# A two-layer decoder trunk on one Trainium2 core: feature tiles computed by three 256-column matmuls per contraction step instead of one of 512 and one of 256, and a pair of tiles in one PSUM bank

## The chip, the core and the metric

The kernel runs on one core of one Trainium2 chip. The metric is the device time of one execution in microseconds, as the median of several. TensorE is called PE here (its weight loads are a row of their own, PEld), VectorE is DVE, ScalarE is ACT, GpSimd is POOL and SyncE, which issues most loads, is SP.

## What is computed

A decoder trunk of two layers on 256 positions of width 2048, in fp32. Each layer has an attention mixer (dilated windows and cross-attention into 256 memory tokens in layer 0, stick-breaking attention and the same cross-attention in layer 1), an output projection, and a gated MLP. Cut to what matters here:

```python
def reference(x, mem, norms, w_in_a, w_o_a, g_kv, w_kv, w_in_b, w_o_b,
              w_mem_kv, w_up, w_conv, b_conv, w_down):
    ...
    h = _rmsnorm(x, nrm[0])
    proj = h @ w_in_a[layer]
    ...

def _conv_ffn(h, w_up, w_conv, b_conv, w_down):
    S = h.shape[1]
    u = h @ w_up
    gate, val = jnp.split(u, 2, axis=-1)
    gp = jnp.pad(gate, ((0, 0), (CONV_WIDTH - 1, 0), (0, 0)))
    acc = b_conv + gp[:, CONV_WIDTH - 1:CONV_WIDTH - 1 + S] * w_conv[CONV_WIDTH - 1]
    for j in range(CONV_WIDTH - 1):
        acc = acc + gp[:, j:j + S] * w_conv[j]
    return (jax.nn.silu(acc) * val) @ w_down
```

The change touches products `h @ w` whose output is wanted with features on the partitions: the queries and keys of both layers, the memory keys, the memory queries, and a part of `h @ w_up`.

## The kernel before

**Three products for one.** An fp32 matrix is held as two float32r parts, high and low. A product of two matrices is high times high, low times high and high times low, summed in PSUM. ACT makes the high part of a weight (line 601, a cast) and DVE the low part (line 602, a subtraction), for pieces of 128x1024. The activations `h` lie in a tile of 16 steps (`kt`, 128 features each) by two parts by 256 positions, so that high and low of one step are 512 columns side by side.

**Feature tiles.** A tile of 128 output features by 256 positions has the weight as the stationary operand and `h` as the moving one, over 16 contraction steps. Before, each step had two matmuls: the weight's high part against both parts of `h` at once (512 columns, line 145, and for the last step line 148), and the weight's low part against the high part of `h` (256 columns, line 146). The 512 columns are a whole PSUM bank: its left half gathers the products with the high part of `h`, its right half those with the low part. So the finished tile is the sum of the two halves: ACT copies the right half out (line 149), and DVE adds the left half (line 150). Each tile takes a bank of its own, out of four called `ps_g`.

**Pairs.** `ws_pair` calls `ws_tile` for two tiles with a common 128x2x256 output, and may multiply the pair by a row of norms (line 188). `narrow`, at the start of each MLP, makes its gate and value tiles so and multiplies the gates by the norm in `gate` (line 829).

**Beside the wide products.** Five groups of 512 features of each MLP are made by `wide`, with fewer products of another form (line 128, all of 512 columns, in seven banks: four `ps_g` and three `ps_s`). Between its matmuls `ws_beside` makes the eight feature tiles of the next group, in two halves of eight contraction steps per round of `wide`; its matmuls are on line 163, its copy and addition on lines 175 and 176, and its bank is the one `ps_s` bank left. Here every instruction is pinned: PE, ACT, DVE and SP run them in the order in which the code writes them. What belongs to a finished pair (gate, convolution, SiLU, product, split) is put on a list, `behind`, of which `catch_up` takes one step twice a round; steps that prepare sums of `h` (lines 585 to 594, 293) are on the same list at the start of a layer's first wide group.

**Counts.** There are 160 feature tiles, 80 by `ws_tile` and 80 by `ws_beside`. That is 2560 contraction steps, each of one 512-column and one 256-column matmul. Everywhere else a scheduler orders the instructions; in `wide` the code does.

Of the kernel before, what the change touches and what calls it, by code (L numbers as in the profile page):

```python
# [14 lines left out]
ALU = mybir.AluOpType  # L15
AX = mybir.AxisListType

P = 128
D = 2048
S = 256  # L20
# [4 lines left out]
KT = D // P  # L25
# [20 lines left out]
class Body:  # L46
# [49 lines left out]
    def pin(self, ins):  # L96
        return self.tc.keep_in_program_order(ins) if self.pinned else ins
# [32 lines left out]
        mm(out, llo, rhi, start=False, stop=False)  # L130
        mm(out, lhi, rlo, start=False, stop=stop)

    def ws_tile(self, out, src, h):


        mm, nc = self.nc.tensor.matmul, self.nc
        b = self.bank()
        self.step()
        for half, (whi, wlo) in enumerate(self.piece(src)):
            for k in range(8):  # L140
                kt = half * 8 + k
                ks = slice(k * P, (k + 1) * P)
                both, one = h[2][:, kt, :, :].rearrange("p a t -> p (a t)"), h[0][:, kt, :]
                if kt < KT - 1:
                    mm(b, whi[:, ks], both, start=kt == 0, stop=False)  # L145
                mm(b[:, 0:S], wlo[:, ks], one, start=False, stop=False)  # L146
                if kt == KT - 1:
                    mm(b, whi[:, ks], both, start=False, stop=True)  # L148
        nc.scalar.copy(out, b[:, S:])
        nc.vector.tensor_add(out, b[:, 0:S], out)  # L150

    def ws_beside(self, out, src, h, done=None):


        raw = self.sb.tile([P, 2048], F32, name="raw", tag="raw", bufs=3)
        self.pin(self.nc.sync.dma_start(raw, src))
        parts = []
        for i in range(2):
            parts.append([self.sb.tile([P, 1024], F32R, name=k, tag=k, bufs=4) for k in ("whi", "wlo")])
            self.split(*parts[i], raw[:, i * 1024:(i + 1) * 1024])  # L160
            yield
        b = self.bank("s")
        mm = lambda *o, **k: self.pin(self.nc.tensor.matmul(*o, **k))  # L163
        for half, (whi, wlo) in enumerate(parts):
            for k in range(8):
                kt = half * 8 + k
                ks = slice(k * P, (k + 1) * P)
                both, one = h[2][:, kt, :, :].rearrange("p a t -> p (a t)"), h[0][:, kt, :]
                if kt < KT - 1:
                    mm(b, whi[:, ks], both, start=kt == 0, stop=False)  # L170
                mm(b[:, 0:S], wlo[:, ks], one, start=False, stop=False)
                if kt == KT - 1:
                    mm(b, whi[:, ks], both, start=False, stop=True)
            yield
        self.pin(self.nc.scalar.copy(out, b[:, S:]))  # L175
        self.pin(self.nc.vector.tensor_add(out, b[:, 0:S], out))  # L176
        if done:
            done()

    def ws_pair(self, src, h, out=None, before=None, R=None):  # L180

        out = self.pairtile() if out is None else out
        for j in range(2):
            if before:
                before(j)
            self.ws_tile(out[:, j, :], src[j], h)
        if R is not None:
            self.nc.vector.tensor_tensor(out, out, R().unsqueeze(1).to_broadcast([P, 2, S]), op=ALU.mult)
        return out

    def as_mm(self, banks, parts, lhs, pi, tiles=(0, 1)):

# [530 lines left out]
    def ffn(self, layer, h, each, filler=None, done=None, late=None):  # L723
        nc = self.nc
        up, uw, dn = (self.a["%s%d" % (k, layer)] for k in ("up", "uw", "dn"))
        r, R = {}, []
# [12 lines left out]
        def spread():  # L739
            if len(R) == 1:  # L740
                R.append(self.spread(R[0], "R"))
            return R[1]

        s, make = self.sums_of_h(h)
# [25 lines left out]
        def weights(ft):  # L770
            return [self.cols[:, cv + i * NFT + ft:cv + i * NFT + ft + 1] for i in range(4)]

        def conv(p, ga):

            pin, c = self.pin, self.pairtile()

            def straight():
                for j in range(2):
                    w = weights(2 * p + j)
                    pin(nc.scalar.activation(c[:, j, :], ga[:, j, :], AF.Identity, scale=w[2], bias=w[3]))  # L780

            def shifted():
                for j in range(2):
                    w = weights(2 * p + j)
                    for i in (1, 0):
                        d = 2 - i
                        pin(nc.vector.scalar_tensor_tensor(c[:, j, d:], ga[:, j, :S - d], w[i], c[:, j, d:],
                                                           op0=ALU.mult, op1=ALU.add))

            def silu():  # L790
                pin(nc.scalar.activation(c, c, AF.Silu))
                if layer == 0 and p == 2 * WIDE[-1] + 1:

                    self.tc.keep_in_program_order(
                        nc.scalar.preload_act_table_set("natural_log_exp_and_others"))

            return c, (straight, shifted, silu)

        def keep(p, c, val):

            g, o = p // 2, p % 2 * 2
            part = lambda i: room[g][i][:, o:o + 2, :]

            def product():
                self.pin(nc.vector.tensor_tensor(c, c, val, op=ALU.mult))

            def high():
                if g not in acts:
                    acts[g] = []
                    room[g] = self.sh([P, 4, S], F32R), self.sh([P, 4, S], F32R)  # L810
                self.pin(nc.scalar.copy(part(0), c))

            def low():
                self.pin(nc.vector.tensor_sub(part(1), c, part(0).bitcast(F32)))
                hi, lo = room[g]
                acts[g] += [(hi[:, o + j, :], lo[:, o + j, :]) for j in range(2)]

            return product, high, low

        def at_once(steps):  # L820
            for step in steps:
                step()

        room = {}
        place = lambda p: p - 2 * sum(v < p // 2 for v in WIDE)

        def gate(ga):
            Rb = spread().unsqueeze(1).to_broadcast([P, 2, S])
            self.pin(nc.vector.tensor_tensor(ga, ga, Rb, op=ALU.mult))

        def narrow(g):
            for p in (2 * g, 2 * g + 1):
                if p == 0:
                    ahead.extend(self.first_sums(uw[0], u) for u in range(2))
                w = place(p)
                ga = self.ws_pair(up[w, 0], h)
                if p == 0:

                    val = self.ws_pair(up[w, 1], h)
                gate(ga)  # L840
                c, steps = conv(p, ga)
                at_once(steps)
                if p:
                    val = self.ws_pair(up[w, 1], h)
                at_once(keep(p, c, val))

        def beside(g):

            st = {}

            def tile(p, i, j):
                if (i, j) == (0, 0):
                    st[p] = [self.pairtile() for _ in range(2)]
                ga, val = st[p]

                def done():
                    if i == 0:
                        st["c"], steps = conv(p, ga)
                        self.behind_this(lambda: gate(ga), *steps)
                    else:  # L860
                        self.behind_this(*keep(p, st["c"], val))

                return self.ws_beside(st[p][i][:, j, :], up[place(p), i][j], h, done if j else None)

            return [lambda p=p, i=i, j=j: tile(p, i, j)
                    for p in (2 * g, 2 * g + 1) for i in range(2) for j in range(2)]

        def turned(g, made, i):
# [12 lines left out]
            at_once(keep(2 * g + i, c, both[1]))  # L881

        narrow(0)
        made = []

# [316 lines left out]
```

## Time and profile before

| what | us |
|---|---|
| time, median of 3 runs (2202.1 to 2207.01) | 2202.43 |
| the profiled execution | 2204.87 |
| its span, first to last instruction | 2203.1 |
| PE busy (10962 matmuls) | 2184.6 |
| PEld busy (weight loads) | 1837.5 |
| DVE busy | 1651.4 |
| ACT busy | 1296.0 |
| POOL busy | 149.1 |

A row of a group of instructions names line, engine and operation, the tiles it writes and reads, its shapes and count, then its busy time in us, the mean duration of one in ns, and the engine's idle time before it with what ended it. A matmul's recorded duration holds its way through the array, so that one begins before the one before it has ended: how fast a stream of matmuls runs is read from the distance between starts. A row of the timeline or of the chain of waits gives a start in us, a duration, and what ran.

### The profile page before, as it was taken

The numbers are of one execution on the slowest core, as the hardware profiler recorded it, in microseconds if no ns is written. First come the engines' busy times: TensorE is split into PE (matmuls) and PEld (weight loads), VectorE is DVE, ScalarE is ACT, GpSimd is POOL, SyncE is SP. The second block draws the span as 40 slices with busy tenths as digits, with TensorE's granted clock in tenths as the row PEclk, the third lists the DMA queues.
The fourth block names the chain that finished last, engine by engine and source line by source line (L and its number), as shares of the span: only waits on it lengthen the run. The fifth ranks groups of instructions, "written<-read, shape, count | busy, mean of one in ns | idle before, by whom it ended". The sixth has DMA issues, their size and how long they took to land.

```text
span 2203.1 us, 28992 instructions
## 1 busy us (share of the span) xinstructions
PE 2184.6 (99%) x10962; PEld 1837.5 (83%) x10962; DVE 1651.4 (75%) x2175; ACT 1296.0 (59%) x1844; POOL 149.1 (7%) x168
## 2 busy tenths in 40 slices
PE   9999999999999999999999999999999999999998
PEld 7888888888888888888888888878888888888886
DVE  6566767987787868778874677569878878687886
ACT  7545656656565665665664554455666656656563
POOL 0000000010101001010100000000101010110100
PEclk9999999999999999999999999999999999999999
DMA  8755557696979979797745444576969798797974
GB/s 320 268 179 179 183 172 248 206 279 221 286 233 283 267 221 295 232 283 257 260 172 191 153 172 165 188 240 203 279 215 293 234 280 264 233 296 225 284 242 181
DMA packets 102380, 516.78 MB, mean 235 GB/s; under 512 B 10464, under 2 KB 10848, under 8 KB 61920
## 3 DMA queue, kind: packets, MB, share of 16 engines
q1 hardware_dynamic: 72288, 439.43, 56.1%
q0 software_dynamic: 29952, 75.51, 17.2%
q8 instruction: 86, 1.41, 0.2%
q14 instruction: 54, 0.44, 0.1%
HBM read 491.82 MB, written 23.07 MB: 234 GB/s over the span
## 4 chain that ended last, share of the span: by engine, by line
PE 96%; DVE 2%; issue 1%; DMA 0%; SPq 0%; ACT 0%; POOL 0%; POOLq 0%; DVEq 0%; ACTq 0%
PE ps_g L128 42%; PE ps_s L163 20%; PE ps_g L145 13%; PE ps_s L128 10%; PE ps_g L146 7%; PE ps_g L148 1%; PE ps_s L876 1%; DVE wlo L602 1%; PE ps_s L279 1%; DMA raw<-in_wmv_dram 0%; PE ps_s L330 0%; PE ps_s L357 0%; PE ps_s L436 0%; PE ps_s L393 0%; PE ps_s L454 0%
## 5 line engine op out<-in xcount | busy, mean ns | idle before, releaser
L602 DVE TENSOR_TENSOR wlo<-raw,whi 128x1024 fp32r<-128x1024 f32 (+1 forms) x758 | 867.0, 1163 | 337.1 <-ACT whi L601 328.5
L601 ACT CAST whi<-raw 128x1024 fp32r<-128x1024 f32 (+1 forms) x758 | 751.4, 1004 | 437.5 <-PE ps_g L128 207.3
L163 PE MATMUL ps_s<-h,whi 128*128 128x512 f32 x1280 | 462.6, 398 | 2.4 <-DVE qk L176 2.4
L128 PE MATMUL ps_g<-whi,sh 128*128 128x512 f32 x1488 | 464.3, 393 | 0.0
L145 PE MATMUL ps_g<-h,whi 128*128 128x512 f32 x1200 | 430.3, 401 | 0.8 <-DVE h L269 0.8
L163 PE MATMUL ps_s<-h,wlo 128*128 128x256 f32 x1280 | 347.1, 281 | 1.2 <-DVE wlo L602 1.1
L146 PE MATMUL ps_g<-h,wlo 128*128 128x256 f32 x1280 | 345.7, 280 | 0.0
L128 PEld LDWEIGHTS ps_g<-whi,sh 128*128 128x128 f32 x1488 | 277.6, 188 | 57.4
L128 PE MATMUL ps_g<-wlo,sh 128*128 128x512 f32 x744 | 291.7, 392 | 0.0
L163 PEld LDWEIGHTS ps_s<-h,whi 128*128 128x128 f32 x1280 | 241.2, 188 | 55.2 <-ACT x L601 3.2
L128 PE MATMUL ps_g<-whi,h 128*128 128x512 f32 x880 | 275.4, 394 | 0.6 <-ACT whi L601 0.6
L145 PEld LDWEIGHTS ps_g<-h,whi 128*128 128x128 f32 x1200 | 225.4, 188 | 52.1 <-DVE h L269 1.1
L163 PEld LDWEIGHTS ps_s<-h,wlo 128*128 128x128 f32 x1280 | 242.3, 189 | 16.0 <-DVE wlo L602 2.3
L146 PEld LDWEIGHTS ps_g<-h,wlo 128*128 128x128 f32 x1280 | 241.5, 189 | 6.4
L602 DVE TENSOR_TENSOR x<-sh,x 128x1024 fp32r<-128x1024 f32 x160 | 189.2, 1219 | 0.0
L128 PEld LDWEIGHTS ps_g<-whi,h 128*128 128x128 f32 x880 | 159.0, 188 | 34.3 <-ACT whi L601 1.1
L128 PE MATMUL ps_g<-wlo,h 128*128 128x512 f32 x440 | 172.8, 393 | 1.1 <-DVE wlo L602 1.0
L128 PEld LDWEIGHTS ps_g<-wlo,sh 128*128 128x128 f32 x744 | 139.7, 188 | 32.5
L601 ACT CAST x<-sh 128x1024 fp32r<-128x1024 f32 x160 | 160.8, 1050 | 0.3 <-DVE sh L647 0.3
L609 POOL DMA_DIRECT2D sh<-in_uw_dram x80 | 97.8, 1226 | 673.4 <-DMA sh<-in_uw_dram 347.7
L175 ACT COPY qk<-ps_s 128x256 f32<-128x256 f32 x80 | 29.9, 374 | 186.1 <-PE ps_s L163 186.1
L128 PE MATMUL ps_g<-x,h 128*128 128x512 f32 x480 | 137.6, 394 | 0.0
(180 smaller groups left out, 2135.8 us busy)
## 6 DMA issues: line engine op xcount, KB each, us to landing
raw<-in_up_dram SPq DMA_DIRECT2D x96, 1024.0 KB, 6.1
raw<-in_dn_dram SPq DMA_DIRECT2D x88, 1024.0 KB, 5.8
raw<-in_uw_dram SPq DMA_DIRECT2D x80, 768.0 KB, 7.3
sh<-in_uw_dram SPq DMA_DIRECT2D x80, 512.0 KB, 8.1
sh<-in_uw_dram POOLq DMA_DIRECT2D x80, 512.0 KB, 10.6
raw<-in_wqk_a_dram SPq DMA_DIRECT2D x24, 1024.0 KB, 4.8
yout<-sh POOLq DMA_DIRECT2D x32, 512.0 KB, 8.6
raw<-in_wo_b_dram SPq DMA_DIRECT2D x16, 1024.0 KB, 4.9
```

Of the source, the lines that this page charges most:

```text
L128: mm = lambda *o, **k: self.pin(self.nc.tensor.matmul(*o, **k))
L145: mm(b, whi[:, ks], both, start=kt == 0, stop=False)
L146: mm(b[:, 0:S], wlo[:, ks], one, start=False, stop=False)
L148: mm(b, whi[:, ks], both, start=False, stop=True)
L163: mm = lambda *o, **k: self.pin(self.nc.tensor.matmul(*o, **k))
L175: self.pin(self.nc.scalar.copy(out, b[:, S:]))
L279: self.nc.tensor.transpose(b[:, k * S + t * P:k * S + (t + 1) * P], self.x[:, t, kt * P:(kt + 1) * P], self.ident)
L601: high = self.pin(self.nc.scalar.copy(hi, of))
L602: low = self.pin(self.nc.vector.tensor_sub(lo, of, hi.bitcast(F32)))
L609: self.nc.gpsimd.dma_start(d.rearrange("p (a n) -> p a n", a=2), src[u][:, 1536:].unsqueeze(1).to_broadcast([P, 2, 512]), accum_op=ALU.add)
L876: nc.tensor.transpose(b[:, j * S + t * P:j * S + (t + 1) * P], of[t][:, f:f + P], self.ident)
```

## The change

Each contraction step of a feature tile becomes three matmuls of 256 columns into the same 256 columns of PSUM: weight high by `h` high, weight low by `h` high, weight high by `h` low. The sum of the three products is then complete in PSUM. Two tiles of a pair lie side by side in one bank, and one instruction takes the bank out: an ACT copy of 128x512, or, where the pair is multiplied by the norm, that DVE multiplication reading PSUM. The copy and addition for each tile go. In `ws_beside` the bank is taken at the pair's first tile, nothing is taken out after that tile, and the gate multiplication comes at once behind the pair's last matmul, where before it was a step on the list `behind`.

```diff
-    def ws_tile(self, out, src, h):
+    def ws_part(self, out, parts, h, half):
...
+        mm = lambda *o, **k: self.pin(self.nc.tensor.matmul(*o, **k))
+        whi, wlo = parts
+        for k in range(8):
+            kt = half * 8 + k
+            ks = slice(k * P, (k + 1) * P)
+            mm(out, whi[:, ks], h[0][:, kt, :], start=kt == 0, stop=False)
+            mm(out, wlo[:, ks], h[0][:, kt, :], start=False, stop=False)
+            mm(out, whi[:, ks], h[1][:, kt, :], start=False, stop=kt == KT - 1)
...
-        nc.scalar.copy(out, b[:, S:])
-        nc.vector.tensor_add(out, b[:, 0:S], out)
...
+        for j in range(2):
+            if before:
+                before(j)
+            self.step()
+            for half, parts in enumerate(self.piece(src[j])):
+                self.ws_part(b[:, j * S:(j + 1) * S], parts, h, half)
+        b = b.rearrange("p (j t) -> p j t", j=2)
+        if R is None:
+            self.nc.scalar.copy(out, b)
+        else:
+            self.nc.vector.tensor_tensor(out, b, R().unsqueeze(1).to_broadcast([P, 2, S]), op=ALU.mult)
+        return out
...
-        self.pin(self.nc.scalar.copy(out, b[:, S:]))
-        self.pin(self.nc.vector.tensor_add(out, b[:, 0:S], out))
-        if done:
-            done()
...
+        if j == 0:
+            st["b"] = self.bank("s")
+        for half in range(2):
+            self.ws_part(st["b"][:, j * S:(j + 1) * S], parts[half], h, half)
             yield
+        if j:
+            done(st["b"].rearrange("p (j t) -> p j t", j=2))
...
-                def done():
+                def done(b):
                     if i == 0:
+                        gate(ga, b)
                         st["c"], steps = conv(p, ga)
-                        self.behind_this(lambda: gate(ga), *steps)
+                        self.behind_this(*steps)
                     else:
+                        self.pin(nc.scalar.copy(val, b))
                         self.behind_this(*keep(p, st["c"], val))
```

In the changed kernel all matmuls of feature tiles are on line 135, the pair's copy and multiplication on lines 156 and 158, gate and copy of the tiles beside `wide` on lines 817 and 850, and the split of weights on lines 589 and 590.

On PE, at the first pair of memory keys in layer 0, these are the rows before, from the end of one tile into the next (`ps_g_287` and `ps_g_342` are two banks, `whi` and `wlo` the parts of a weight, `h1` the activations):

```order
L145 MATMUL ps_g_287<-h1_84,whi_294 128x512
L146 MATMUL ps_g_287<-h1_84,wlo_295 128x256 x2
L148 MATMUL ps_g_287<-h1_84,whi_294 128x512
L145 MATMUL ps_g_342<-h1_84,whi_345 128x512
L146 MATMUL ps_g_342<-h1_84,wlo_346 128x256
```

The same place after the change:

```order
L135 MATMUL ps_g_277<-h1_84,whi_294 128x256 x2
L135 MATMUL ps_g_277<-h1_84,wlo_295 128x256
L135 MATMUL ps_g_277<-h1_84,whi_294 128x256
L135 MATMUL ps_g_277<-h1_84,whi_358 128x256
L135 MATMUL ps_g_277<-h1_84,wlo_359 128x256
```

Every step has three matmuls of 256 columns now, and the second tile goes on in the bank of the first. What stands between the feature tiles on PE has kept its place, but for a few matmuls at three points.

On DVE, where the first wide group of layer 0 goes over from its first tile beside to the second, these are the rows before (`wlo<-raw,whi` is the low part of a weight, `qk` the pair's output or a scratch pair, `x<-sh,x` the low part of a sum of weights; the rows from `qk<-h` to the last `qk<-qk` and the one on `h_3298` prepare sums of `h`):

```order
L293 TENSOR_TENSOR h_3298<-qk,h_3298 128x4x128
L590 TENSOR_TENSOR qk<-h_2654 128x512
L592 TENSOR_TENSOR qk<-qk 128x128
L585 SCALAR_TENSOR_TENSOR qk<-qk 128x128
L594 TENSOR_TENSOR qk<-qk 128x128
L585 SCALAR_TENSOR_TENSOR qk<-qk 128x128
L176 TENSOR_TENSOR qk<-ps_s,qk 128x256
L602 TENSOR_TENSOR wlo<-raw,whi 128x1024 x2
L602 TENSOR_TENSOR x<-sh,x 128x1024 x2
```

And after:

```order
L281 TENSOR_TENSOR h_3800<-qk,h_3800 128x4x128
L578 TENSOR_TENSOR qk<-h_3100 128x512
L580 TENSOR_TENSOR qk<-qk 128x128
L573 SCALAR_TENSOR_TENSOR qk<-qk 128x128
L582 TENSOR_TENSOR qk<-qk 128x128
L573 SCALAR_TENSOR_TENSOR qk<-qk 128x128
L590 TENSOR_TENSOR wlo<-raw,whi 128x1024 x2
L590 TENSOR_TENSOR x<-sh,x 128x1024 x2
```

The addition that took the first tile out of the one free bank (line 176) is gone from between the sums and the split of the next weight; nothing has come in its place.

More of the change, by code (lines that the diff above doesn't have):

```diff
@@ L131, in mm3, with ws_pair, ws_beside @@
         mm(out, lhi, rlo, start=False, stop=stop)
-    def ws_tile(self, out, src, h):
-        mm, nc = self.nc.tensor.matmul, self.nc
-        b = self.bank()
[L138 to L148, printed above, removed]
-        nc.scalar.copy(out, b[:, S:])
-        nc.vector.tensor_add(out, b[:, 0:S], out)
-    def ws_beside(self, out, src, h, done=None):
+    def ws_part(self, out, parts, h, half):
[7 more added lines that the diff above has]
+            mm(out, whi[:, ks], h[1][:, kt, :], start=False, stop=kt == KT - 1)
+    def ws_pair(self, src, h, out=None, before=None, R=None):
+        out = self.pairtile() if out is None else out
+        b = self.bank()
+        for j in range(2):
[10 more added lines that the diff above has]
+        return out
+    def ws_beside(self, src, h, st, j, done):
         raw = self.sb.tile([P, 2048], F32, name="raw", tag="raw", bufs=3)
@@ L161, in ws_beside @@
             yield
[L162 to L173, printed above, removed]
-            yield
-        self.pin(self.nc.scalar.copy(out, b[:, S:]))
-        self.pin(self.nc.vector.tensor_add(out, b[:, 0:S], out))
-        if done:
-            done()
[L180 to L189, printed above, removed]
+        if j == 0:
+            st["b"] = self.bank("s")
+        for half in range(2):
+            self.ws_part(st["b"][:, j * S:(j + 1) * S], parts[half], h, half)
+            yield
+        if j:
+            done(st["b"].rearrange("p (j t) -> p j t", j=2))
     def as_mm(self, banks, parts, lhs, pi, tiles=(0, 1)):
@@ L825, in ffn, with gate @@
         place = lambda p: p - 2 * sum(v < p // 2 for v in WIDE)
-        def gate(ga):
+        def gate(ga, of):
             Rb = spread().unsqueeze(1).to_broadcast([P, 2, S])
-            self.pin(nc.vector.tensor_tensor(ga, ga, Rb, op=ALU.mult))
+            self.pin(nc.vector.tensor_tensor(ga, of, Rb, op=ALU.mult))
         def narrow(g):
@@ L835, in narrow @@
                 w = place(p)
-                ga = self.ws_pair(up[w, 0], h)
                 if p == 0:
-                    val = self.ws_pair(up[w, 1], h)
-                gate(ga)
+                    ga, val = (self.ws_pair(up[w, i], h) for i in range(2))
+                    gate(ga, ga)
+                else:
+                    ga = self.ws_pair(up[w, 0], h, R=spread)
                 c, steps = conv(p, ga)
@@ L854, in tile @@
                 ga, val = st[p]
-                def done():
+                def done(b):
                     if i == 0:
+                        gate(ga, b)
                         st["c"], steps = conv(p, ga)
-                        self.behind_this(lambda: gate(ga), *steps)
+                        self.behind_this(*steps)
                     else:
+                        self.pin(nc.scalar.copy(val, b))
                         self.behind_this(*keep(p, st["c"], val))
-                return self.ws_beside(st[p][i][:, j, :], up[place(p), i][j], h, done if j else None)
+                return self.ws_beside(up[place(p), i][j], h, st, j, done)
             return [lambda p=p, i=i, j=j: tile(p, i, j)
```

## Prediction, made before the changed kernel ran

> **What bounds the kernel now.** I read the page first, engine totals and the chain of waits by engine:
>
> ```profile
> PE 2184.6 (99%) x10962; PEld 1837.5 (83%) x10962; DVE 1651.4 (75%) x2175; ACT 1296.0 (59%) x1844; POOL 149.1 (7%) x168
> PE 96%; DVE 2%; issue 1%; DMA 0%; SPq 0%; ACT 0%; POOL 0%; POOLq 0%; DVEq 0%; ACTq 0%
> ```
>
> PE is busy 99% of the span and carries 96% of the chain. The view of waits, of PE alone, says how little it waits for others:
>
> ```profile
> PE ps_s L163 <- DVE qk L176: 2.4, 2, 1.2
> PE ps_s L279 <- DVE x L528: 2.1, 1, 2.1
> ...
> PE ps_s L163 <- DVE wlo L602: 1.1, 2, 0.6
> PE ps_g L128 <- DVE wlo L602: 1.0, 2, 0.5
> ```
>
> With the shorter ones it is under 10 us. So a change in DVE's or ACT's work is worth a few us at most, and a change in how fast matmuls follow each other is worth its full size. The groups to be changed:
>
> ```profile
> L163 PE MATMUL ps_s<-h,whi 128*128 128x512 f32 x1280 | 462.6, 398 | 2.4 <-DVE qk L176 2.4
> L145 PE MATMUL ps_g<-h,whi 128*128 128x512 f32 x1200 | 430.3, 401 | 0.8 <-DVE h L269 0.8
> L163 PE MATMUL ps_s<-h,wlo 128*128 128x256 f32 x1280 | 347.1, 281 | 1.2 <-DVE wlo L602 1.1
> L146 PE MATMUL ps_g<-h,wlo 128*128 128x256 f32 x1280 | 345.7, 280 | 0.0
> ```
>
> With 80 on line 148, that is 2560 steps of 512 + 256 columns. Each becomes 3 x 256: the same 768 columns, 2560 more matmuls and 2560 more weight loads. The durations (398, 281 ns) overlap and price nothing; starts do. The chain of waits in order of time, at the end of a memory-key tile and into the stream of line 128 behind it, gives starts and durations from start to start:
>
> ```profile
> 49.82 0.23 PE ps_g L145
> 50.06 0.12 PE ps_g L146
> 50.17 0.24 PE ps_g L145
> ...
> 52.65 0.23 PE ps_g L145
> 52.88 0.24 PE ps_g L146 x2
> 53.12 0.24 PE ps_g L148
> 53.36 27.21 PE ps_g L128 x120
> ```
>
> From 49.82 to 52.65 lie eight steps: 2.83 us, 354 ns a step, of which some 0.235 us for the 512 columns and 0.118 for the 256. The last step's order was turned, and so two 256-column matmuls stand in a row there: 0.24 us for two.
>
> **The stream of matmuls.** Three matmuls of 256 columns in a row stand nowhere in this trace; two do, 160 times. At another tile's end and at one beside the wide products, the timeline of PE:
>
> ```profile
> 404.11 0.40 PE L146 MATMUL ps_g<-h,wlo 128*128 128x256 f32 x2
> 404.34 0.40 PE L148 MATMUL ps_g<-h,whi 128*128 128x512 f32 x1
> ...
> 463.61 0.40 PE L163 MATMUL ps_s<-h,wlo 128*128 128x256 f32 x2
> 463.84 0.39 PE L163 MATMUL ps_s<-h,whi 128*128 128x512 f32 x1
> ```
>
> That is 0.23 us for two in both, beside 0.24 above: 0.115 to 0.12 us each, with a weight load under each. I take the middle, rounded up, 0.118: a third one in a row finds what the second found. Three make 354 ns, against 354 (49.82 to 52.65) or, over more steps, a little less: from the turned step at 404.34 to that of two tiles later
>
> ```profile
> 415.64 0.40 PE L148 MATMUL ps_g<-h,whi 128*128 128x512 f32 x1
> ```
>
> are 11.30 us for 32 steps, 353 ns. So 3 x 118 - 353 = +1 ns a step, x 2560 = +2.6 us. The ends: at 0.115 it is -8 ns a step, -20 us; at 0.12, +7 ns, +18 us.
>
> Can the weight load keep up? After a wait the pipeline is empty and shows a load by itself:
>
> ```profile
> 1470.70 0.19 PEld L145 LDWEIGHTS ps_g<-h,whi 128*128 128x128 f32 x1 [1.08 <-DVE h L269]
> 1470.70 0.50 PE L145 MATMUL ps_g<-h,whi 128*128 128x512 f32 x1 [0.85 <-DVE h L269]
> 1470.81 0.19 PEld L146 LDWEIGHTS ps_g<-h,wlo 128*128 128x128 f32 x1
> 1471.04 0.27 PE L146 MATMUL ps_g<-h,wlo 128*128 128x256 f32 x1
> ```
>
> The second load starts 0.11 us after the first, so a load takes about 0.11, just under the 0.118 of a 256-column matmul. It fits with nothing to spare, three times in a row where it was two.
>
> The Trainium skill, "TensorE: Matmul & The Clock Gate", section "Back-to-back issue gap", speaks against this change: a warm matmul takes its columns at 2.4 GHz plus about 2.5 ns, whatever its width. An estimate by it: 2560 more matmuls cost 2560 x 2.5 = +6.4 us, and the sum below would be higher by 3.8 us. The trace's 0.235 for 512 columns is twice its 0.118 for 256, so a fixed part does not show at this resolution; the absolute times are longer than the rule's.
>
> **What goes from ACT and DVE.** The copies and additions, and the rows nearest to what replaces them:
>
> ```profile
> L176 DVE TENSOR_TENSOR qk<-ps_s,qk 128x256 f32<-128x256 f32 x80 | 33.9, 424 | 85.5 <-ACT qk L175 85.0
> L175 ACT COPY qk<-ps_s 128x256 f32<-128x256 f32 x80 | 29.9, 374 | 186.1 <-PE ps_s L163 186.1
> L829 DVE TENSOR_TENSOR qk<-qk,R 128x512 f32<-128x512 f32 x24 | 16.5, 686 | 0.1
> L545 DVE TENSOR_TENSOR sh<-ps_g,sc 128x512 f32<-128x512 f32 x16 | 11.0, 685 | 7.8 <-ACT junk L244 7.8
> L764 ACT COPY sh<-ps_g 128x512 f32<-128x512 f32 x64 | 36.7, 585 | 26.9 <-PE ps_g L128 26.9
> ```
>
> DVE loses 160 additions at 0.424, 68 us; its pair multiplications read PSUM instead of SBUF at the same price (685 against 686 ns). ACT loses 160 copies at 0.374, 60 us, and gains 42 at 0.585, 25 us (80 pairs less 38 that DVE takes out). All this lies beside PE's stream, so I cost it at nothing for the end; if PE waited for the splits throughout it would be worth up to 68 us, but the waits above say it does not. Nobody waits longer for a pair: ACT's 0.374 then DVE's 0.424 become one 0.585 or 0.685. Behind the gate's multiplication in the pinned order stand the splits of the next weight, where the addition stood, which waited for ACT as well; the convolution behind it moves up by one call of `catch_up`, and nobody on PE waits for it. Banks come free once a pair, so the next tile of the same pair waits for none.
>
> One wait goes, at the start of each layer's first wide group. The timeline there, of layer 0:
>
> ```profile
> 432.06 0.86 PE L128 MATMUL ps_s<-x,h 128*128 128x512 f32 x3
> ...
> 433.35 0.28 DVE L585 SCALAR_TENSOR_TENSOR qk<-qk 128x128 f32<-128x128 f32 x1
> 433.55 0.41 DVE L176 TENSOR_TENSOR qk<-ps_s,qk 128x256 f32<-128x256 f32 x1
> 433.88 2.35 DVE L602 TENSOR_TENSOR wlo<-raw,whi 128x1024 fp32r<-128x1024 f32 x2
> 434.11 0.47 PE L163 MATMUL ps_s<-h,whi 128*128 128x512 f32 x1 [1.19 <-DVE qk L176]
> 435.15 0.39 PE L163 MATMUL ps_s<-h,wlo 128*128 128x256 f32 x1 [0.57 <-DVE wlo L602]
> ```
>
> PE waits for the addition, because the second tile needs the one bank; then for the low part, which DVE makes behind the addition. Without the addition the first wait is gone, but the second is next: the low part comes earlier by only 433.88 - 433.55 = 0.33 us, and the first matmul fills little of the time. So -0.4 us in each layer, -0.8 in all. Behind the same wait in layer 1 the clock that PE was granted is halved, as the view by windows says (the 0.50 after the five engines; the other columns are their busy us and counts, then DMA):
>
> ```profile
> 1532.40:1535.70 3.30, 3.30 (x12) 2.82 (x12) 3.30 (x4) 0.00 (x0) 0.00 (x0) 0.50 0.93 232
> ```
>
> That cost 3.3 x 0.5 = 1.7 us, and layer 0 had none for the same wait; I leave it, as +-1.7.
>
> **The sum.** 2204.87 (the profiled execution, 2203.1 of span and 1.8 around it) + 2.6 - 0.8 = 2206.7. The median of the runs is 2.4 us below that execution, so 2204.3; I say 2204. A measurement of this kernel can tell about 0.3%, 6.6 us, from no change, and this is within it.
>
> **Rivals.**
>
> Slower: each matmul has a fixed cost, which the starts at a tile's end do not show because two in a row are absorbed by what stands around them. For it: line 128's stream takes 10.99 us for 48 in the chain,
>
> ```profile
> 1074.00 10.99 PE ps_g L128 x48
> ```
>
> 229 ns for 512 columns, so 768 columns in 1.5 matmuls take 343.5; the feature tiles take 353 in two. If that half matmul more is what costs the 9.5 ns, one costs 19, and 2560 cost +49 us: 2251. It decides once the third of three takes over 0.12. Against it: the two in a row at 0.115 to 0.12, where it wants 0.124, and 0.24 for line 148's 512 columns, where it wants 0.229; by these the tiles' stream is slow by the column. 24%, with whatever lies between.
>
> Slower by another way: the load of weights, 0.11 us, starts only once the matmul before has begun; with 0.02 for the hand-over a step would take 390 ns, +95 us, 2296. The 0.115 already holds a load and its hand-over, twice in a row: 4%.
>
> Faster: matmuls of one width run undisturbed. The 120 of line 128 above take 27.21 / 120 = 0.227 us each; half of it is 0.1134, three make 340, -13 ns a step, -33 us: 2168; at half of 0.229, -24 us: 2177. For it: the stream of one width is the faster one by the column, and the feature tiles become such a stream. Against: line 148's matmul, with 512 columns behind it as well, takes 0.24 like those of line 145, so it may be reading `h` that is slow, and that stays. 20%.
>
> **How the numbers follow.** The forecast's case holds 52%: 40 of it within 0.3%, and 12 slower, since 0.12 gives +18 us. Slower by over 0.3% is 12 + 24 + 4 = 40%, within 40%, faster 20%. The range reaches down to 2174, which leaves out the lower end of the faster case, 6%, and up to 2248, which leaves out the end of the first slower case and the second, 14%.
>
> **What would show it.** In the profile after: 13522 matmuls and as many weight loads; DVE busy about 1584 us, ACT about 1261. Right, if the timeline inside a tile shows starts 0.117 to 0.12 apart, three to a step of 0.35, and tiles of 5.65 us. 0.124 and 5.95 us a tile say fixed cost; 0.113 and 5.45 say the faster case; 0.13 says the weight load. At the first wide group PE should wait for line 590's low part alone, until some 0.3 us earlier in DVE's run. The prediction is wrong altogether if PE shows waits for ACT or DVE at the ends of pairs, for it leaves no room for them.

## The result, and the profile after

| | before | after |
|---|---|---|
| median of 4 runs each, us | 2203.61 (2202.1 to 2207.01) | 2217.42 (2217.05 to 2217.7) |
| profiled execution, us | 2204.87 | 2217.7 |
| its span, us | 2203.1 | 2215.7 |

The ratio of after to before is 1.0067, with a 95% interval of 1.0054 to 1.0079: the change makes the kernel slower by 13.8 us. That is more than the 6.6 us that a measurement can tell from no change.

The page of the changed kernel begins with the engine totals and the chain by engine:

```profile
PE 2201.0 (99%) x13522; PEld 1971.6 (89%) x13522; DVE 1597.4 (72%) x2015; ACT 1290.3 (58%) x1726; POOL 149.3 (7%) x168
PE 97%; DVE 1%; issue 1%; DMA 0%; ACT 0%; SPq 0%; POOL 0%; POOLq 0%; DVEq 0%; ACTq 0%
```

DVE's and ACT's counts and busy times fell; PE stands at 99% as before, and its share of the chain has grown by a point. The view of waits, of PE alone, has four rows (us in total, times, the longest):

```profile
PE ps_s L267 <- DVE x L516: 2.1, 1, 2.1
PE ps_g L128 <- ACT whi L589: 2.1, 2, 1.1
PE ps_s L965 <- DVE ones L959: 1.2, 1, 1.2
PE ps_s L135 <- DVE wlo L590: 0.4, 2, 0.2
```

The wait of 2.4 us for the addition into `qk` is gone, and of the waits for the low part of a weight 0.4 us are left where there were 2.1. The wait for the cast of a weight grew to 2.1 us; before it was

```profile
PE ps_g L128 <- ACT whi L601: 0.6, 1, 0.6
```

All eight rows of the view before add up to 9.5 us and these four to 5.8, so PE waits less than before, and the kernel is slower all the same: the time has gone into the matmuls themselves. The chain in order of time, at the second group of wide products in layer 0, first before and then after (start, us, what; "x16" and "x24" are the matmuls of one half of a tile, eight contraction steps):

```profile
456.50 2.82 PE ps_s L163 x16
...
461.42 2.81 PE ps_s L163 x16
```

```profile
454.75 2.87 PE ps_s L135 x24
457.62 0.69 PE ps_g L128 x3
458.32 0.68 PE ps_s L128 x3
459.00 0.69 PE ps_g L128 x3
459.69 0.69 PE ps_s L128 x3
460.38 2.86 PE ps_s L135 x24
```

Half a tile took 2.815 us here and takes 2.865 us. There are 160 such halves beside the wide products; over the 146 that hold no wait in either trace, from the first start to that of the next matmul behind, the mean went from 2.812 to 2.867 us, and for 160 that is +8.9 us. The other half of the steps stands in tiles by themselves; the chain there, after the change:

```profile
389.97 12.12 PE ps_g L135 x101
```

101 matmuls in 12.12 us are 0.120 us each. A pair of tiles is 96 of them, 11.52 us, where the two tiles before took the 11.30 us that the prediction worked out. Of the 160 half tiles by themselves 124 hold no wait; their mean, taken in the same way, went from 2.815 to 2.867 us, and for 160 that is +8.3 us. The two together are about +17 us.

The view of the chain at the first two pairs of memory keys shows a smaller price:

```profile
31.85 22.73 PE ps_g L135 x192
```

192 matmuls in 22.73 us are 0.1184 us each. Inside 23 of the 80 tiles by themselves, all memory keys among them, the matmuls go at this pace. Inside the others, and inside all 80 beside the wide products, they go at 0.120.

**What was won back.** At the first wide group of layer 0, the timeline of PE, before and then after (start, duration, what ran, and in brackets the wait ahead of it):

```profile
424.35 0.64 PE L128 MATMUL ps_g<-whi,h 128*128 128x512 f32 x2
425.49 0.50 PE L128 MATMUL ps_g<-wlo,h 128*128 128x512 f32 x1 [0.50 <-DVE wlo L602]
...
427.22 0.39 PE L163 MATMUL ps_s<-h,whi 128*128 128x512 f32 x1
...
430.00 0.85 PE L128 MATMUL ps_g<-x,h 128*128 128x512 f32 x3
```

```profile
430.68 0.63 PE L128 MATMUL ps_g<-whi,h 128*128 128x512 f32 x2
431.15 0.39 PE L128 MATMUL ps_g<-wlo,h 128*128 128x512 f32 x1
...
432.78 0.28 PE L135 MATMUL ps_s<-h,whi 128*128 128x256 f32 x1
...
435.65 0.86 PE L128 MATMUL ps_g<-x,h 128*128 128x512 f32 x3
...
438.41 0.28 PE L135 MATMUL ps_s<-h,whi 128*128 128x256 f32 x1
438.57 0.39 PE L135 MATMUL ps_s<-h,wlo 128*128 128x256 f32 x1
```

The first block of wide products took 424.35 to 427.22, 2.87 us, and takes 2.10 us; the second took 430.00 to 434.11 (the row with the 1.19 us of wait, in the prediction), 4.11 us, and takes 435.65 to 438.41, 2.76 us; the half tile behind it went from 3.70 to 3.01 us. That is -2.8 us in layer 0. In layer 1 the same three places give -4.4 us, of which 1.7 us are the halved clock that stood there; but the clock is halved for 3.4 us elsewhere in layer 1 now, so this part is no gain. About -5.5 us are. The reason stands in DVE's timeline after the change:

```profile
437.30 2.35 DVE L590 TENSOR_TENSOR wlo<-raw,whi 128x1024 fp32r<-128x1024 f32 x2
```

The split of the next weight starts 1.1 us before the wide block ends at 438.4; before, it started 1.1 us after that point (433.88, where the three matmuls from 432.06 on leave PE free at 432.75). DVE is 2.2 us further ahead of PE. The run split_only below, with the new matmuls and the old copies and additions, tells the two parts of the change apart: there the split starts 0.9 us after that point (439.14, where PE is free at 438.27), so 2.0 of the 2.2 us come with the new taking-out, that is with additions gone from the work before this group as well. The first block takes 2.10 us in split_only too, so its gain came with the slower matmuls. From split_only to the changed kernel the three places give -3.9 us in the two layers together; the other -1.5 or so of the -5.5 us are the stream's.

**What else was lost.** At ten places, once in each wide group, a new short wait stands at the first step behind a pair that was taken out. The timeline after the change, of ACT, DVE and PE together:

```profile
468.25 0.59 ACT L851 COPY qk<-ps_s 128x512 f32<-128x512 f32 x1 [3.18 <-PE ps_s L135]
468.73 2.00 ACT L589 CAST whi<-raw 128x1024 fp32r<-128x1024 f32 x2
469.81 2.36 DVE L590 TENSOR_TENSOR wlo<-raw,whi 128x1024 fp32r<-128x1024 f32 x2 [3.62 <-ACT whi L589]
...
470.81 0.28 PE L135 MATMUL ps_s<-h,whi 128*128 128x256 f32 x1
471.09 0.39 PE L135 MATMUL ps_s<-h,wlo 128*128 128x256 f32 x1
471.32 0.40 PE L135 MATMUL ps_s<-h,whi 128*128 128x256 f32 x2
```

The copy of the pair (line 851) takes 0.59 us where that of a tile took 0.37, the casts stand behind it, DVE's low part waits for them, and PE's second matmul comes 0.28 us after the first in place of 0.12. The chain has 3.13 us for this half (470.97 to the end of 23 more matmuls at 474.10) against 2.86 without a wait, so the ten cost about 2.7 us. In split_only, where the copies of 0.37 us stay, the second matmul comes after 0.12 us at these places. A longer wait of this kind, 0.5 us, stands at the second pair of each layer's first wide group; before, one of the two places had 0.3 us.

At the start, the load that the chain goes through lands later:

```profile
4.49 8.85 DMA raw<-in_wmv_dram
```

It was 7.76 us, so +1.1 us; the change touches nothing ahead of it, and its cause is open.

The account, by the distance from each start on PE to the next one: tiles by themselves +9.3 us, tiles beside the wide products +9.1, the matmuls on line 128 -5.0 (-4.3 of them at the first wide groups), all other matmuls -0.9, with the +1.1 at the start in it. Behind the last matmul it is +0.1. The sum, +12.6, is the difference of the spans. The halved clock costs 1.7 us in both, at different places.

### The profile page after: what moved, and what is told of

Read it like the earlier page. It is cut to its first block, busy times and chain, and to the rows that moved or that the text cites. A ratio compares the mean times of both kernels' runs of the same rounds, so it can differ in the third digit from the quotient of the medians.

```text
span 2215.7 us, 33889 instructions
## 1 busy us (share of the span) xinstructions
PE 2201.0 (99%) x13522; PEld 1971.6 (89%) x13522; DVE 1597.4 (72%) x2015; ACT 1290.3 (58%) x1726; POOL 149.3 (7%) x168
## 4 chain that ended last, share of the span: by engine, by line
PE 97%; DVE 1%; issue 1%; DMA 0%; ACT 0%; SPq 0%; POOL 0%; POOLq 0%; DVEq 0%; ACTq 0%
PE ps_g L128 42%; PE ps_g L135 21%; PE ps_s L135 20%; PE ps_s L128 10%; PE ps_s L867 1%; PE ps_s L267 1%; DVE wlo L590 1%; DMA raw<-in_wmv_dram 0%; PE ps_s L318 0%; PE ps_s L345 0%; PE ps_s L424 0%; PE ps_s L482 0%; PE ps_s L442 0%; PE ps_s L381 0%; DVE x L590 0%
## 5 line engine op out<-in xcount | busy, mean ns | idle before, releaser
L135 PE MATMUL ps_s<-h,whi 128*128 128x256 f32 x2560 | 485.4, 282 | 0.0
L135 PE MATMUL ps_g<-h,whi 128*128 128x256 f32 x2560 | 470.6, 284 | 0.0
L135 PEld LDWEIGHTS ps_s<-h,whi 128*128 128x128 f32 x2560 | 408.7, 191 | 7.1
L135 PEld LDWEIGHTS ps_g<-h,whi 128*128 128x128 f32 x2560 | 400.1, 191 | 0.8 <-ACT h L256 0.2
L135 PE MATMUL ps_s<-h,wlo 128*128 128x256 f32 x1280 | 363.1, 284 | 0.5 <-DVE wlo L590 0.4
L135 PE MATMUL ps_g<-h,wlo 128*128 128x256 f32 x1280 | 361.6, 283 | 0.0
L589 ACT CAST x<-sh 128x1024 fp32r<-128x1024 f32 x160 | 167.1, 1050 | 27.2 <-PE ps_s L128 20.9
L128 PE MATMUL ps_s<-x,h 128*128 128x512 f32 x480 | 135.9, 391 | 0.0
```

What stands on the lines that cost most here:

```text
L589: high = self.pin(self.nc.scalar.copy(hi, of))
```

## The experiments

The theory after the result was that the third matmul of each step is dearer than what it took away; the question was what sets 0.12 us for a matmul of 256 columns. Candidates were a fixed cost for each matmul, the load of its weights, and the three products that go into the same columns.

### Fewer columns: w224 and w128

The changed kernel with all steps of a tile but the first at 224 columns, and the same at 128 (`n = S if kt == 0 else 128`).

```diff
-            mm(out, whi[:, ks], h[0][:, kt, :], start=kt == 0, stop=False)
-            mm(out, wlo[:, ks], h[0][:, kt, :], start=False, stop=False)
-            mm(out, whi[:, ks], h[1][:, kt, :], start=False, stop=kt == KT - 1)
+            n = S if kt == 0 else 224
+            mm(out[:, 0:n], whi[:, ks], h[0][:, kt, 0:n], start=kt == 0, stop=False)
+            mm(out[:, 0:n], wlo[:, ks], h[0][:, kt, 0:n], start=False, stop=False)
+            mm(out[:, 0:n], whi[:, ks], h[1][:, kt, 0:n], start=False, stop=kt == KT - 1)
```

> The changed kernel, but 15 of 16 contraction steps of every feature tile use matmuls of 224 columns instead of 256; the last 32 positions of these tiles are left incomplete. In the changed kernel the starts of these matmuls are 0.12 us apart. Theory 'load': the distance is the weight load under each matmul, so it stays at 0.12 and the time stays near 2217 us. Rival 'columns': it is the columns alone, 0.469 ns each, so it falls to 0.105 and 7200 matmuls save 108 us: 2109. Rival 'fixed': some 17 ns fixed and 0.4 ns a column: 0.107, 2123.

> As the run with 224 columns, with 128 in 15 of 16 steps: the last 128 positions of the feature tiles are left incomplete. Theory 'load': the distance cannot fall below the weight load, 0.11 us by the pair of loads after a wait: 0.11 to 0.12, time 2145 to 2217 us. Rival 'columns': 0.06, -432 us: 1785, unless the splits on ACT and DVE bind before. Rival 'fixed': 0.068, 1843.

Measured: 2189.4 us and 2187.24 us, one run each. In both the clock is halved at more places than before (mean granted clock 0.995 and 0.991 against 0.998), so the starts say more, read where the clock is full; the timeline of PE inside a tile, at 224 and then at 128 columns:

```profile
40.77 0.27 PE L135 MATMUL ps_g<-h,wlo 128*128 128x224 f32 x1
40.88 0.39 PE L135 MATMUL ps_g<-h,whi 128*128 128x224 f32 x2
...
42.11 0.27 PE L135 MATMUL ps_g<-h,wlo 128*128 128x224 f32 x1
```

```profile
40.84 0.27 PE L135 MATMUL ps_g<-h,wlo 128*128 128x128 f32 x1
40.95 0.39 PE L135 MATMUL ps_g<-h,whi 128*128 128x128 f32 x2
...
42.18 0.27 PE L135 MATMUL ps_g<-h,wlo 128*128 128x128 f32 x1
```

In both, twelve matmuls (four steps) take 1.34 us: 0.112 us each, whether they have 224 columns or 128. At 224 columns that is none of the three values expected: the load was to keep 0.12, and the rivals gave 0.105 and 0.107. At 128 it is what the load was to give (0.11 to 0.12), and far from the rivals' 0.06 and 0.068. So there is a floor that the columns don't set, and each matmul here has one thing more that doesn't depend on its columns: the load of 128x128 weights. The prediction had 0.11 us for such a load, from two behind a wait. The Trainium skill, "TensorE: Matmul & The Clock Gate", section "LDWEIGHTS (loading the stationary operand)", has a load take one cycle of 1.2 GHz for each of its columns, 107 ns for 128; the measured floor is 5 ns above it. That the floor is the load, and not another fixed time, was argued and not shown. At 256 columns a matmul takes 0.120, so this floor is near, but by the wider streams below it is not what sets the time there.

### More columns: w288, w384 and both512

The changed kernel with 288 and with 384 columns to each matmul, and the kernel before with 512 columns for both products of a step. Each makes a stream of one width.

```diff
+            wide = h[2][:, kt, :, :].rearrange("p a t -> p (a t)")
+            mm(out, whi[:, ks], wide[:, 0:288], start=kt == 0, stop=False)
+            mm(out, wlo[:, ks], wide[:, 0:288], start=False, stop=False)
+            mm(out, whi[:, ks], wide[:, 224:512], start=False, stop=kt == KT - 1)
```

```diff
-                if kt < KT - 1:
-                    mm(b, whi[:, ks], both, start=kt == 0, stop=False)
-                mm(b[:, 0:S], wlo[:, ks], one, start=False, stop=False)
-                if kt == KT - 1:
-                    mm(b, whi[:, ks], both, start=False, stop=True)
+                mm(b, whi[:, ks], both, start=kt == 0, stop=False)
+                mm(b, wlo[:, ks], both, start=False, stop=kt == KT - 1)
```

> The changed kernel, with 288 columns instead of 256 in every matmul of a feature tile, the second tile's columns overlapping the first's (the tiles' values are not those of the reference). Theory 'load': the load is covered by now, and the columns alone show, 0.128 to 0.132 us a matmul, +58 to +92 us: 2275 to 2309. Rival 'columns': 0.135, +115 us: 2332. Rival 'fixed': 0.133, +98 us: 2315.

> The changed kernel with 384 columns in every matmul of a feature tile, overlapping (the tiles' values are not those of the reference). Theory 'mixing' (13.3 ns and 0.417 a column): 0.1733 us a matmul, three of one width, +410 us: 2627 us. Rival 'reading h' (0.46 a column): 0.177, +438 us: 2655 us.

> The kernel before with the weight's low part also against both parts of h: two matmuls of 512 columns a step, one width only (it adds the product of the two low parts, which the reference's rounding hides). Theory 'mixing': 0.2267 us a matmul, 453 ns a step, +257 us: 2460 us. Rival 'reading h': 0.235 a matmul, 470 ns a step, +300 us: 2503 us.

Measured: 2317.0, 2632.14 and 2463.68 us, one run each. The chain in order of time, of the three in this order:

```profile
430.00 25.42 PE ps_g L135 x192
```

```profile
437.69 24.98 PE ps_g L135 x144
```

```profile
501.23 3.63 PE ps_s L160 x16
```

| columns | us | matmuls | ns for one |
|---|---|---|---|
| 256 (after) | 12.12 | 101 | 120.0 |
| 288 | 25.42 | 192 | 132.4 |
| 384 | 24.98 | 144 | 173.5 |
| 512 | 3.63 | 16 | 226.9 |

From 256 to 512 columns it is (226.9 - 120.0) / 256 = 0.418 ns for a column, and 120.0 - 256 x 0.418 = 13 ns that don't depend on the columns. By this line 384 columns take 173.5, as measured, and 288 take 133.4, measured 132.4. So 288 met the expectation of 'fixed' (2315 us), and 384 and 512 columns met those of 'mixing' (2627 and 2460 us) and not those of 'reading h'. In a stream of one width at these places a matmul costs 13 ns beside its columns, and the rows of the prediction didn't show it.

The second thing that follows: 512 and 256 columns would take 226.9 + 120.0 = 347 ns by this table, and a step of the kernel before took 353 (11.30 us for 32). So the stream that changes its width at each matmul is 6 ns a step slower here. The change pays 13 ns for one more matmul and gets these 6 back: 7 ns a step, and 2560 steps make +17 to +18 us, the size that the two traces gave.

The line doesn't hold inside the 23 tiles with the other pace. There 288 columns take 25.60 / 192 = 133.3 ns, as the chain of that kernel has it,

```profile
32.29 25.60 PE ps_g L135 x192
```

beside 118.4 for 256, and 512 columns take 0.233 us in both512. By these two ends only 3 or 4 ns would be fixed, and 384 columns would take 176; they take 173.4 there as elsewhere. A step of the kernel before took 353 there too, and 3 x 118.4 = 355, so that the change costs only 2 ns a step. The same 23 tiles are apart in split_only, adjacent and both512, and 20 of them in w288; at 384 columns, and at 224 and 128, they are like the others. Why is open.

### One width without the new taking-out: split_only

The kernel before, whose tile keeps its bank, its copy and its addition; only the matmuls are the change's.

```diff
-                if kt < KT - 1:
-                    mm(b, whi[:, ks], both, start=kt == 0, stop=False)
-                mm(b[:, 0:S], wlo[:, ks], one, start=False, stop=False)
-                if kt == KT - 1:
-                    mm(b, whi[:, ks], both, start=False, stop=True)
+                mm(b[:, 0:S], whi[:, ks], h[0][:, kt, :], start=kt == 0, stop=False)
+                mm(b[:, 0:S], wlo[:, ks], h[0][:, kt, :], start=False, stop=False)
+                mm(b[:, S:], whi[:, ks], h[1][:, kt, :], start=False, stop=kt == KT - 1)
```

> The kernel before with the change's matmuls alone: three of 256 columns a step, the third into the right half of the bank, so that a bank a tile, the copy on ACT and the addition on DVE stay. Theory: the stream of matmuls is the whole loss, and the merged taking-out is worth only the wait at the two first wide groups and the like, 1 to 5 us: 2218 to 2222 us. Rival: the taking-out was worth more, some 10 us that hide a larger loss of the stream: over 2226. Rival: the one bank's longer holding cost time that shows as part of the loss: under 2216.

Measured: 2223.3 us (2222.04 to 2223.65, 4 runs), 1.0093 of before (1.0076 to 1.0109). The chain and, at the first half of a tile, the timeline of PE:

```profile
456.33 2.87 PE ps_s L160 x24
```

```profile
461.80 0.28 PE L160 MATMUL ps_s<-h,whi 128*128 128x256 f32 x1
461.92 0.34 PE L160 MATMUL ps_s<-h,wlo 128*128 128x256 f32 x1
462.10 0.40 PE L160 MATMUL ps_s<-h,whi 128*128 128x256 f32 x2
```

The half tile takes 2.87 us, as after the whole change, though the third product goes into other columns here. So it isn't that three products go into the same columns; the time comes with the number of matmuls. The kernel is 5.9 us slower than the changed one and missed its expectation by some 1 to 5 us: at the first step of 66 of the 80 tiles beside the wide products the third matmul comes 0.18 us after the second in place of 0.12, and the tile's first half takes 0.06 to 0.07 us more, 4.5 us in all. That matmul writes the right half of the bank, but it isn't the copy of the tile before that it waits for: here the copy had ended 2.5 us earlier,

```profile
459.24 0.37 ACT L169 COPY qk<-ps_s 128x256 f32<-128x256 f32 x1 [2.18 <-PE ps_s L160]
```

and its cause is open. With these matmuls the new taking-out is thus worth 5.9 us against the old one: it gains these 4.5 us and the 3.9 us at the first wide groups, and loses the 2.7 us of the ten waits.

### The same matmuls in another order: grouped8 and grouped2

The kernel before, with eight products of 512 columns in a row and then eight of 256 (grouped8), or two and two (grouped2); the last product of 512 columns of each tile stays at its end. No work is added or left out.

```diff
-            for k in range(8):
-                kt = half * 8 + k
...
+            for k0 in range(0, 8, 8):
+                group = [(half * 8 + k, slice(k * P, (k + 1) * P)) for k in range(k0, k0 + 8)]
...
+                for kt, ks in group[:-1] if end else group:
+                    mm(b, whi[:, ks], both(kt), start=kt == 0, stop=False)
+                for kt, ks in group:
+                    mm(b[:, 0:S], wlo[:, ks], h[0][:, kt, :], start=False, stop=False)
+                if end:
+                    mm(b, whi[:, ks], both(kt), start=False, stop=True)
```

> The kernel before, with the order of its matmuls turned inside each half of a tile: first the eight of 512 columns (weight high), then the eight of 256 (weight low). Theory 'mixing': a matmul costs 13.3 ns and 0.417 ns a column (0.12 at 256 in the changed kernel, 0.1333 at 288, 0.2267 at 512), a step of 512 + 256 should take 347 ns, and the 353 of the kernel before are lost at each change of width; in groups of eight the loss is nearly gone: some 6 ns a step less, -14 us, 2190 us. Rival 'reading h': columns that are read from the activations' tile are slow by the column, 0.46 ns, in any order: no change, 2203 to 2204 us.

> As grouped8, in groups of two steps: 512, 512, 256, 256. Theory 'mixing': half of the changes of width are gone, so half of the loss: -8 us, 2196 us. Rival 'reading h': no change.

Measured: grouped8 2194.86 us (2194.59 to 2195.41, 5 runs), 0.9961 of before (0.9947 to 0.9975); grouped2 2195.91 us (2194.01 to 2197.64, 6 runs), 0.9967 (0.9955 to 0.9979). The chain of grouped8, beside the wide products:

```profile
465.00 2.79 PE ps_s L164 x16
...
469.88 2.77 PE ps_s L164 x16
```

and in a tile by itself, away from the 23 odd ones:

```profile
409.47 1.83 PE ps_g L145 x8
411.31 0.95 PE ps_g L147 x8
```

Eight steps take 2.78 us in these rows (1.83 + 0.95), 347 ns a step. Over all half tiles without a wait, those beside the wide products went from 2.812 to 2.778 us, and those by themselves from 2.815 to 2.801 only. That part of the theory holds: grouped by width, the same work takes less time. Its size came out at about half: 8 us of the 14 expected from grouped8. And the trace of the kernel before says that a change of width doesn't bring the loss by itself. Of its half tiles by themselves, away from the odd ones, 42 of 111 go at 346 to 347 ns a step with all their changes, as these two rows, eleven steps apart, show:

```profile
193.05 0.40 PE L145 MATMUL ps_g<-h,whi 128*128 128x512 f32 x1
...
196.87 0.39 PE L145 MATMUL ps_g<-h,whi 128*128 128x512 f32 x1
```

The others go at 352 to 355. Likewise grouped2, with four times the changes of grouped8, is as fast. What makes the loss is open. These two are the fastest versions found, 0.4% and 0.3% under before and 1% under after.

### The same weights twice in a row: adjacent

The changed kernel with the two products of the high part next to each other.

```diff
-            mm(out, wlo[:, ks], h[0][:, kt, :], start=False, stop=False)
-            mm(out, whi[:, ks], h[1][:, kt, :], start=False, stop=kt == KT - 1)
+            mm(out, whi[:, ks], h[1][:, kt, :], start=False, stop=False)
+            mm(out, wlo[:, ks], h[0][:, kt, :], start=False, stop=kt == KT - 1)
```

> The changed kernel with the two matmuls of the weight's high part next to each other, the low part's third. Theory: a matmul of 256 columns costs its 0.12 us whatever is loaded under it, and loading the same weights twice in a row saves nothing; but the low part is wanted 0.24 us after the step's start instead of 0.12, so the ten short waits of PE for it, 0.17 us each at the first step behind a taken-out value pair in the wide groups, go or shrink: 2215 to 2217 us. Rival: a repeated load of the same weights is shorter or left out: starts under 0.12 apart after the first, 2190 to 2210 us. Rival: the ten waits were not for the low part: no change, 2217 to 2218 us.

Measured: 2219.27 us (2218.83 to 2220.47, 5 runs), 1.0073 of before (1.0059 to 1.0087). The timeline of PE behind a pair that was taken out:

```profile
472.13 0.39 PE L135 MATMUL ps_s<-h,whi 128*128 128x256 f32 x2
472.41 0.38 PE L135 MATMUL ps_s<-h,wlo 128*128 128x256 f32 x1
472.64 0.40 PE L135 MATMUL ps_s<-h,whi 128*128 128x256 f32 x2
```

The low part is wanted one matmul later, and the low part's matmul comes 0.28 us after the step's start, where 0.24 would be two matmuls: the wait of about 0.17 us is 0.05 us. That is -1.2 us for the ten, as the wait's cause demands. The whole missed the 2215 to 2217 us expected: the first load took 0.7 us longer again and other small things the rest, and against the changed kernel's 2217.42 us nothing can be told apart. Matmuls stay 0.120 us apart, and 2190 to 2210 us didn't come, so having the same weights twice in a row saves nothing here.

## Why the prediction was off by 13 us, point by point

The measured time is inside the range, at the slow end of the case that the forecast was made from. The likeliest value, no change, was wrong. The range, 2174 to 2248 us, held the forecast's case and most of two rivals, so that the time lies in it says little.

- **PE sets the end, DVE and ACT are cover.** Right. DVE fell by 54 us of busy time (68 were forecast) and ACT's instructions by 118, and the time went up. ACT's busy time was to be 1261 us and is 1290.3: the 42 copies are there at 0.585 us, but rows of other work are busy longer; not followed up.
- **"A third one in a row finds what the second found", 0.118 us.** The step that failed, by its size. It was 0.1184 inside 23 tiles, the first memory keys among them, from which the prediction's 2.83 us for eight steps was read, and 0.120 elsewhere; a tile takes 5.76 us (5.68 at the odd ones) and not 5.65. Elsewhere a third one doesn't find what the second found: in grouped8, behind its products of 512 columns, the next start comes 113 ns after the first matmul of 256 columns, 119 after the second and 120 after each later one (means over 237 half tiles). Of the 0.23 us for two that the prediction read beside the wide products, the first had 113 ns and the second 120. 0.12 was its upper end, priced at +18 us; the traces gave +17.
- **"A fixed part does not show at this resolution."** It was there, 13 ns for a matmul by widths of 256 to 512, at most places. What hid it was the comparison of 0.118 with 0.235 at one of the odd places, where streams of one width too take 118.4 and 233. The rule of the Trainium skill in "TensorE: Matmul & The Clock Gate", section "Back-to-back issue gap", which it gives for an isolated matmul, has the right form and, by the column, the right size: 0.418 ns measured, 1 / 2.4 GHz = 0.417 by the rule. Its 2.5 ns for each matmul is a fifth of what the runs here show, for matmuls that each load their own weights.
- **The weight load fits with nothing to spare.** Right, if the floor of 0.112 us is the load: it is 8 ns under 0.120.
- **The first wide group, -0.8 us.** The mechanism was right, the term was mis-sized: about -5.5 us without the clock, -3.9 of them by the taking-out. The sum moved DVE only by the one addition before the split, 0.33 us. It left out that DVE sheds additions all the way there and comes to this place 2.0 us ahead, and that slower matmuls give the splits more time.
- **"Nobody waits longer for a pair."** It failed at ten places, 2.7 us. The prediction had named waits at the ends of pairs as what would show it wrong altogether; they came, but they are a small part of the 13.8 us. The argument looked at the copy and addition of one tile against one copy of a pair; the queue behind the longer copy on ACT was not looked at, nor that PE wants the low part 0.12 us earlier, as the matmul ahead of it has 256 columns in place of 512.
- **The rivals.** The fixed cost was the right mechanism at most places, with 13 ns in place of 19; as the end of the mixed stream paid half of it back, it is 7 ns a step net and not 19, +17 and not +49 us. The undisturbed stream of one width was half true: one width does save, 6 ns a step where the mixed stream took 353, but the extra matmul costs twice that. 0.1134 for 256 columns, half of 0.227, lacks the fixed part. The weight load that starts late didn't occur; no row shows its 0.02 us for a hand-over.

## What to carry to other kernels

The price of a matmul split in three is read from streams of one width at two sizes: their difference gives the column, what is left the matmul. It has to be read at more than one place: here 23 of 160 tiles gave other numbers. Halving a wide matmul's time, or taking a narrow one's out of a mixed stream, can hide a fixed part of 13 ns, and 2560 of these are 33 us. Where PE is busy 99% of the span, work taken from the other engines pays only at the few places that wait for them; reordering the same matmuls by width was worth 8 us without touching the other engines, and taking 54 us of work from DVE some 6 (2217.4 us against split_only's 2223.3).

## What the runs showed that was not expected

- In a stream of matmuls that each load 128x128 weights, the starts come 0.112 us apart in the mean, with 224 columns as with 128.
- Inside 23 of 160 tiles matmuls run at 118.4 ns for 256 columns and 233 for 512, inside the rest at 120 and 227, in all kernels with these widths; at 384 columns there is no difference. The cause is open.
- The stream of 512 and 256 columns in turn takes 346 to 347 ns a step in some half tiles and 352 to 355 in others. The cause is open.
- The load at the start took 7.76 to 8.27 us in the four kernels with 10962 matmuls (before, grouped8, grouped2, both512) and 8.85 to 9.56 us in five with 13522 (after, split_only, adjacent, w288, w384), with the same instructions ahead of it. Why a longer program should do this was not tried. The longest, of adjacent:

```profile
4.49 9.56 DMA raw<-in_wmv_dram
```
